# A decoder-layer step on one core: block sums and output-weight sums on VectorE, half of the weight steps moved to the second couples, stores on GpSimd's queue, and the first output weights loaded into operand places

## The chip, the core and the metric

The kernel runs on one core of a Trainium2 chip. The core has TensorE (PE, matmuls, with its weight loads shown as PEld), VectorE (DVE), ScalarE (ACT), GpSimd (POOL) and SyncE (SP), which here only issues transfers (DMAs). Every engine works through its own instructions in order. A DMA stands in the queue of the engine that issues it; an issue that has to wait for something holds up what stands behind it on that engine. The metric is the device time of one execution in microseconds (us).

## The reference

One step of a decoder layer on a prompt of 2048 rows and 8 sample rows, in float32, width 1024. Cut to what matters:

```python
hn = rmsnorm(x, g_norm) * (1 + scale) + shift           # scale, shift, gate from c @ w_ada + b_ada
z  = hn @ w_in                                          # (2048, 1024) @ (1024, 5136)
xa, za, q, k, v, glr, zg = split(z)
# group 1: conv4 over xa, two block-diagonal gates, a recurrence h = a*h + u, y_lru = h * silu(za)
# group 2: 4 heads of gated linear attention over chunks, with a state of 128x256 per head,
#          y_gla = rmsnorm(o) * silu(zg)
mix = concat([y_lru, y_gla]) @ w_out                    # (2048, 2048) @ (2048, 1024)
y   = rmsnorm(x + gate * mix, g_final)
```

The states of both groups are outputs too, and the 8 sample rows go through the same layer with states of their own (`state_gla` for group 2).

## The kernel before

Float32 products are made of two float32r parts, a high and a low one: x = hi + lo, three matmuls per product. A *split* makes them: ACT copies (`hi`), DVE subtracts (`lo`). The large products use a scheme with seven block products in place of eight (operands A11, A12, A21, A22 and their sums S1 to S4 on the row side; B11, B12, B21, B22 and combinations T1 to T4 on the weight side).

The prompt is worked on in two halves of 1024 rows. In order of time:

- **First-half heads** (to about 348 us): projections and attention of four heads (`gla_head`). Beside them run the row sums (`sums`, 40 additions on POOL into S1, S2 and, by way of memory, S3, S4), the gate (`ada_gate`), the second half's rows (`second_rows`, which normalizes them and stores eight row operands `fd`) and the gate weights.
- **First-half couples** (to about 628 us): eleven pairs of column blocks (eight `Lru`, three `Zg`), each seven products of 12 matmuls. `couples` interleaves the products of neighbours (list `uses`) and prepares each product's weights five uses ahead (`lead=5`) in one of seven places `op`. For the first half a couple loads raw weights (`load_raw`), splits them, and stores the parts to `wtd`; `combine` also multiplies the 8 sample rows with them (`sample_cols`, L303 and L309).
- **Second-half heads** (to about 939 us): as the first, with a tail of sample work (`sample_state`: loads `vsd` and `state_gla`, ACT scales, DVE adds). Beside them runs `out_weights`: 16 steps, each of which loads four blocks of `w_out` (tile `r`), multiplies them by the gate `g`, makes three sums (tile `t`) on POOL, splits two of them (tile `p`), and stores all to memory (`wd`, `wd2`) for the output projection.
- **Second-half couples** (to about 1166 us): the weights' parts come back from `wtd`.
- **Output projection** (to the end): seven products per pair of row blocks, weights from `wd`, `wd2` in the places `w0` to `w6` (`load_w`).

Work beside the main products is put off by `after(units, fn)` and called by `tick`, which counts the main line's progress; a product of a couple counts half a unit. `with behind(q)` gives an instruction the place behind the latest one of engine q; so `low_dma` puts a DMA behind what SP has at that time. A tile that is written again waits for all readers of its earlier use, stores among them. SP's and ACT's DMAs signal through eight semaphores in turn, so a ninth waits for the first.

Of the kernel before, what the change touches and what calls it, by code (L numbers as in the profile page):

```python
# [14 lines left out]
P = 128  # L15
# [38 lines left out]
def hybrid_kernel(ctx, tc, i, o):  # L54
# [64 lines left out]
    am = cp.tile([P, 4, P], F32, name="am")  # L119
    V.memset(am, 0.0)  # L120
    amh = cp.tile([P, 4, P], F32R, name="amh")
    aml = cp.tile([P, 4, P], F32R, name="aml")
# [10 lines left out]
    St = [cp.tile([P, DV], F32, name=f"S{h}") for h in range(H)]  # L133
# [3 lines left out]
    g2s = cp.tile([P, H * DK], F32R, name="g2s")  # L137
# [33 lines left out]
    gls = hnp.tile([P, TH + NS], F32R, name="gls")  # L171
# [192 lines left out]
    def take(col, n, k0, nk, raw):  # L364
# [6 lines left out]
        else:  # L371
# [4 lines left out]
            after(0.5, lambda: SP.dma_start(parts[col, k0], both[:, :, c].bitcast(F32)))  # L376
# [394 lines left out]
    def out_weights(hp, pp, then):  # L771


        def begin(q):

            g = hp.tile([P, 2, 256], F32, tag="g", name="g")
# [4 lines left out]
            r = load(8 * q)  # L781

            def add():
                G.tensor_tensor(g, g, bt, op=OP.add)
                step(8 * q, r, g)

            after(1, add)

        def where(s):

            return s // 8, s // 4 % 2, s % 4

        def load(s):
            q, f, m = where(s)
# [7 lines left out]
        def step(s, r, g):  # L802
            t = hp.tile([P, 3, 256], F32, tag="t", name="t", bufs=2)
            b11, b12, b21, b22 = r[:, 0, 0], r[:, 0, 1], r[:, 1, 0], r[:, 1, 1]
            q, f, m = where(s)
            c = slice(q * 256, q * 256 + 256)
            last = s % 8 == 7
            ahead = None if last else load(s + 1)

            def split(n, x):  # L810
                p = pp.tile([P, 2, 256], F32R, tag="p", name="p", bufs=2)
                with behind(S), behind(V):
                    S.copy(p[:, 0], x)
                    V.tensor_tensor(p[:, 1], x, p[:, 0].bitcast(F32), op=OP.subtract)
                return lambda: low_dma(wd2[2 * f + n, :, :, m, c], p.bitcast(F32))

            def store():
                for x, k in ((r.rearrange("p a b n -> p (a b) n"), 0), (t, 4)):
                    y = slice(1 - f, x.shape[1] - f)
                    low_dma(wd[f, k + y.start:k + y.stop, :, m, c].rearrange("k p n -> p k n"), x[:, y])  # L820

            for a in range(2):
                G.tensor_tensor(r[:, a], r[:, a], g, op=OP.mult)
            G.tensor_tensor(t[:, 1], b22, b12, op=OP.subtract)
            G.tensor_tensor(b12, b12, b11, op=OP.subtract)
            G.tensor_tensor(t[:, 0], b22, b12, op=OP.subtract)
            G.tensor_tensor(t[:, 2], b21, t[:, 0], op=OP.subtract)

            def splits():
                keep = split(0, b22 if f else b11), split(1, t[:, 2 * f])  # L830
                after(0.5, lambda: end(keep))

            def end(keep):
                for k in keep:
                    k()
                store()
                if not last:
                    step(s + 1, ahead, g)
                else:
                    after(1, (lambda: begin(1)) if q == 0 else then)  # L840

            after(1, splits)
# [221 lines left out]
    def sample_state(h, smp, b0, st, done, more):  # L1064
# [17 lines left out]
        after(0.5, update)  # L1082
        after(2.5, lambda: sample_out(h, b0, st, s0, done, more), True)

    def sample_out(h, b0, st, s0, done, more):
# [5 lines left out]
        SP.dma_start(o[7][0, b0:b0 + 4, h].rearrange("b k v -> k b v"), s0)  # L1091
# [28 lines left out]
    def sample_heads(k):  # L1120
# [15 lines left out]
        more = (lambda: after(0.5, lambda: sample_heads(k + 1))) if k < 3 else lambda: None  # L1136
# [1292 lines left out]
```

## Time and profile before

| | |
|---|---|
| median of 3 runs | 1507.06 us (1502.69 to 1511.88) |
| the profiled execution | 1506.31 us, its span 1504.3 us |
| PE idle, all of the span | 80.0 us |
| granted PE clock, mean | 0.981 |
| DMA | 340.84 MB, mean 227 GB/s |

The page gives for each engine its busy time, then the span in 40 equal slices of 37.6 us. In the two rows below, each digit is the share of a slice in tenths, 9 for 90% or more:

```profile
DVE  5776775665698888757778574667667686588886
POOL 1351602224313232054364100000002000000000
```

POOL's arithmetic lies in slices 1 to 4 (the sums), 5 to 16 (rows, couples' combinations) and 17 to 22 (the weight steps). DVE is at 8 or 9 in the first-half couples (slices 11 to 15). Further views of the trace are quoted with the prediction: waits (who waited for whom, total us, times, the longest), windows (for each stretch the busy time of the five engines PE, PEld, DVE, ACT, POOL, then granted clock, DMA share, GB/s), timelines (start, duration, engine, line, operation, and in brackets the idle time before it and what ended it), and sources (duration of one line's instructions in ns, least, median and most).

### The profile page before, as it was taken

What the parts mean: (1) busy time and instruction counts of PE and PEld (TensorE: products, weight loads), DVE (VectorE), ACT (ScalarE), POOL (GpSimd) and SP (SyncE); (2) the same over time, 40 slices, a digit from 0 to 9 for tenths busy, and PEclk for the clock granted to TensorE, in tenths of its full rate; (3) what the DMA queues carried; (4) which work ended last, traced back from release to release, by engine and by line L of the source; (5) the groups of instructions that cost most, each with busy time, mean ns of one, the idle gap of its engine ahead of it and who ended that gap; (6) DMA issues with size and microseconds to landing.
All of it is one profiled execution on the core that took longest, in us unless ns stands there. A gap on an engine that the chain in (4) does not pass through costs nothing.

```text
span 1504.3 us, 22504 instructions
## 1 busy us (share of the span) xinstructions
PE 1424.3 (95%) x8113; PEld 1175.7 (78%) x8113; DVE 1072.3 (71%) x2262; ACT 701.7 (47%) x1310; POOL 291.3 (19%) x297
## 2 busy tenths in 40 slices
PE   7989999997999999898999799999999899999997
PEld 5878889786777777778888788778888687777786
DVE  5776775665698888757778574667667686588886
ACT  4524344544675767433444332575663432244332
POOL 1351602224313232054364100000002000000000
PEclk9999999999999999999999899999999999999999
DMA  9625536748668548988878554766579857793452
GB/s 321 261 85 181 203 134 212 242 135 259 230 240 304 208 173 281 327 261 282 284 269 299 164 186 156 247 196 204 181 225 337 359 207 261 260 351 119 145 169 105
DMA packets 196469, 340.84 MB, mean 227 GB/s; under 512 B 12355, under 2 KB 130787, under 8 KB 192638
## 3 DMA queue, kind: packets, MB, share of 16 engines
q1 hardware_dynamic: 163061, 311.87, 60.6%
q10 hardware_dynamic: 31056, 20.19, 4.2%
q0 software_dynamic: 2240, 7.34, 1.2%
q8 instruction: 64, 1.05, 0.3%
q14 instruction: 48, 0.39, 0.1%
HBM read 204.73 MB, written 134.69 MB: 226 GB/s over the span
## 4 chain that ended last, share of the span: by engine, by line
PE 52%; DVE 15%; DMA 15%; issue 9%; ACT 5%; POOL 2%; SPq 1%; ACTq 0%; DVEq 0%; POOLq 0%
PE acc L2067 11%; PE tp L2067 8%; PE acc L1524 4%; PE tp L1524 3%; PE acc L701 3%; PE acc L702 3%; PE acc L703 3%; PE acc L397 2%; PE acc L396 2%; PE acc L395 2%; DMA raw<-in_w_in_dram 2%; DMA wd<-scratch 2%; DMA w<-wd 2%; PE po L1047 1%; DVE tg L1674 1%
## 5 line engine op out<-in xcount | busy, mean ns | idle before, releaser
L1524 PE MATMUL acc<-op,op 128*128 128x512 f32 x1056 | 251.4, 392 | 2.4 <-DMA op<-wtd 2.0
L1524 PEld LDWEIGHTS acc<-op,op 128*128 128x128 f32 x1056 | 198.3, 189 | 46.0 <-ACT op L1304 3.2
L1524 PE MATMUL tp<-op,op 128*128 128x512 f32 x792 | 197.6, 396 | 5.0 <-DVE acc L1534 5.0
L2067 PE MATMUL acc<-w,a 128*128 128x512 f32 (+1 forms) x792 | 189.6, 393 | 5.3 <-DMA w<-wd 4.1
L2067 PEld LDWEIGHTS acc<-w,a 128*128 128x128 f32 x792 | 148.5, 190 | 41.9 <-issue 7.9
L1524 PEld LDWEIGHTS tp<-op,op 128*128 128x128 f32 x792 | 148.6, 190 | 37.5 <-DVE acc L1534 5.9
L395 PE MATMUL acc<-w,op 128*128 128x256 f32 (+1 forms) x508 | 152.2, 300 | 3.2 <-ACT w L373 2.2
L397 PE MATMUL acc<-w,op 128*128 128x256 f32 (+1 forms) x508 | 146.2, 288 | 1.5 <-DVE op L270 1.5
L396 PE MATMUL acc<-w,op 128*128 128x256 f32 (+1 forms) x508 | 145.6, 287 | 0.8 <-DVE w L374 0.8
L2067 PE MATMUL tp<-w,a 128*128 128x512 f32 x564 | 137.2, 393 | 0.0
L2067 PEld LDWEIGHTS tp<-w,a 128*128 128x128 f32 x564 | 105.2, 188 | 28.0 <-issue 5.2
L701 PE MATMUL acc<-op,w 128*128 128x512 f32 x296 | 122.1, 412 | 2.3 <-ACT w L373 2.3
L702 PE MATMUL acc<-op,w 128*128 128x512 f32 x296 | 117.1, 396 | 0.0
L703 PE MATMUL acc<-op,w 128*128 128x512 f32 x296 | 117.0, 395 | 0.0
L395 PEld LDWEIGHTS acc<-w,op 128*128 128x128 f32 x508 | 98.1, 193 | 5.5 <-ACT w L373 2.6
L397 PEld LDWEIGHTS acc<-w,op 128*128 128x128 f32 x508 | 97.7, 192 | 2.1 <-DVE op L270 1.9
L396 PEld LDWEIGHTS acc<-w,op 128*128 128x128 f32 x508 | 97.6, 192 | 2.0 <-DVE w L374 1.1
L227 ACT ACTIVATE junk<-on 128x256 bf16<-128x256 f32 x64 | 26.7, 418 | 134.5 <-DVE on L1052 105.8
L1918 ACT CAST a<-s 128x512 fp32r<-128x512 f32 x61 | 36.5, 620 | 98.4 <-issue 35.8
L1641 DVE SCALAR_TENSOR_TENSOR cv<-xa,vecT,cv 128x512 f32<-128x512 f32 x96 | 73.1, 762 | 11.4 <-ACT cv L1639 10.3
L711 POOL DMA_DIRECT2D mixd<-zs x27 | 20.5, 761 | 304.4 <-DVE zs L1683 266.3
L1048 DVE TENSOR_TENSOR S<-S,pkv 128x256 f32<-128x256 f32 x60 | 25.1, 418 | 72.8 <-PE po L1047 72.4
(424 smaller groups left out, 2900.4 us busy)
## 6 DMA issues: line engine op xcount, KB each, us to landing
wtd<-op SPq DMA_DIRECT2D x77, 512.0 KB
op<-wtd SPq DMA_DIRECT2D x77, 512.0 KB
w<-parts SPq DMA_DIRECT2D x16, 1024.0 KB
a<-mixd SPq DMA_DIRECT2D x63, 256.0 KB
parts<-w SPq DMA_DIRECT2D x15, 1024.0 KB
w<-wd SPq DMA_DIRECT2D x10, 1024.0 KB
wr<-in_w_in_dram SPq DMA_DIRECT2D x18, 512.0 KB
wada<-in_w_ada_dram SPq DMA_DIRECT2D x16, 512.0 KB
```

The lines of the kernel that those rows point to most:

```text
L227: S.activation(junk[:m, :n], x, AF.Square, accum_out=out)
L395: PE.matmul(ps, part(0, kt, c), hi[:, kt % 4], start=kt == 0, stop=False)
L396: PE.matmul(ps, part(0, kt, c), lo[:, kt % 4], start=False, stop=False)
L397: PE.matmul(ps, part(1, kt, c), hi[:, kt % 4], start=False, stop=kt == KT - 1)
L701: PE.matmul(ps[:, :n], hi[:, kt], a, start=kt == 0, stop=False)
L702: PE.matmul(ps[:, :n], hi[:, kt], b, start=False, stop=False)
L703: PE.matmul(ps[:, :n], lo[:, kt], a, start=False, stop=kt == KT - 1)
L1048: V.tensor_tensor(St[h], St[h], pkv, op=OP.add)
L1524: PE.matmul(ps, w[:, u, k], t[:, v, k], start=q < 3 and (k, u, v) == (0, 0, 0), stop=(k, u) == (3, 1), skip_group_check=True)
L1641: V.scalar_tensor_tensor(cv, xa[:, k:k + 512], cw[k], cv, op0=OP.mult, op1=OP.add)
L1918: S.copy(t[:, 0, k], (low(t) if src is None else src)[:, k])
L2067: PE.matmul(ps, t[:, u, k], w[:, v, k, c], start=(q < 3 or ps is own) and (k, u, v) == (0, 0, 0), stop=(k, u) == (3, 1), skip_group_check= ...
```

## The change

Line numbers of the changed kernel are higher by 1 to 41.

- `sums`: its 40 additions go from POOL to DVE, cut into pieces half a unit apart; its stores `sd` go from SP to POOL's queue.
- `out_weights` takes f: the eight steps of f = 0 stay beside the second-half heads (their stores on POOL's queue), the eight of f = 1 run beside the second-half couples (their stores on SP's, tiles in a pool of their own, one buffer `t` in place of two). The arithmetic is on DVE in both.
- Stores that move to POOL's queue: `parts`, `fd`, `sd`, `gated_w`, the sample states `o[7]`, the states `o[4]`. In all POOL issues 127 DMAs in place of 28, SP 605 in place of 684, ACT 61 in place of 77; POOL has 108 tensor operations of two inputs in place of 246, DVE 1199 in place of 1059.
- `second_rows` starts behind `ada_gate`, and its first step waits for the sums (`ready`).
- `couples`: couple 1's raw weights are asked for behind four uses' weights, and its sample columns come behind product 1. One of the `zs` of `Zg(0, 0)` gets a tile of its own.
- Sample states are used 1 unit (was 0.5) and 3 units (was 2.5) after their loads are asked for.
- Output weights: the places are those of the couples' operands (`ops`, tags o0 to o6), free by then; the first weight B11 is loaded behind product (10, 0) of the second-half couples. Small tiles of the projection move into earlier pools.

```diff
-            after(0.5, lambda: SP.dma_start(parts[col, k0], both[:, :, c].bitcast(F32)))
+            after(0.5, lambda: G.dma_start(parts[col, k0], both[:, :, c].bitcast(F32)))
...
-            for a in range(2):
-                G.tensor_tensor(r[:, a], r[:, a], g, op=OP.mult)
-            G.tensor_tensor(t[:, 1], b22, b12, op=OP.subtract)
...
+        def step(q, m, r, g):
+            t = hp.tile([P, 3, 256], F32, tag="t", name="t", bufs=2 - f)
...
+            with behind(V):
+                for a in range(2):
+                    V.tensor_tensor(r[:, a], r[:, a], g, op=OP.mult)
+
+            def combine():
+                with behind(V):
+                    V.tensor_tensor(t[:, 1], b22, b12, op=OP.subtract)
+                    V.tensor_tensor(b12, b12, b11, op=OP.subtract)
+                    V.tensor_tensor(t[:, 0], b22, b12, op=OP.subtract)
+                    V.tensor_tensor(t[:, 2], b21, t[:, 0], op=OP.subtract)
+                after(0.5, high)
...
+            def store(ps):
+                put = low_dma if f else G.dma_start
...
+                    after(0.5 if f else 1, lambda: step(q, m + 1, ahead[0], g))
...
-        after(0.5, update)
-        after(2.5, lambda: sample_out(h, b0, st, s0, done, more), True)
+        after(1, update)
+        after(3, lambda: sample_out(h, b0, st, s0, done, more), True)
...
-        SP.dma_start(o[7][0, b0:b0 + 4, h].rearrange("b k v -> k b v"), s0)
+        G.dma_start(o[7][0, b0:b0 + 4, h].rearrange("b k v -> k b v"), s0)
...
-            S.dma_start(fd[0:4, :, k, p * P:(p + 1) * P].rearrange("o p c -> p o c"), f)
+            G.dma_start(fd[0:4, :, k, p * P:(p + 1) * P].rearrange("o p c -> p o c"), f)
...
-            after(1, lambda: SP.dma_start(fd[4:8, :, k, p * P:(p + 1) * P].rearrange("o p c -> p o c"), b))
+            G.dma_start(fd[4:8, :, k, p * P:(p + 1) * P].rearrange("o p c -> p o c"), b)
...
-            add_up(s1, [(h21, None), (h22, OP.add), (l21, OP.add), (l22, OP.add)])
-            add_up(s2, [(s1, None), (h11, OP.subtract), (l11, OP.subtract)])
+            with behind(V):
+                add(s1, h21, h22)
+                add(s1, s1, l21)
...
         def zs(self):
-            if self.more:
-                return self.more.pop(0)()
+            own = self.more.pop(0) if self.more else None
+            if own:
+                return own()
...
         cs[0].load_raw()
-        for u in range(lead):
+        for u in range(lead - 1):
             prepare(u, True)
+        cs[1].load_raw()
+        if cs[1].src is not None:
+            prepare(lead - 1)
         for u, (m, q) in enumerate(uses):
             cs[m].product(q)
...
+            if u == 1 and cs[1].src is None:
+                prepare(lead - 1)
             prepare(u + lead)
...
+    zg0 = Zg(0, 0)
+    zg0.more = [None] * 3 + [lambda: lp.tile([P, 512 + 4], F32, tag="xa", name="zs")[:, :512]]
...
+    after(3, lambda: out_weights(1, owp, owp, lambda: lp.tile([P, 2, 256], F32, tag="t2", name="g"), lambda: done.append(1)))
...
-    couples([Lru(1, j) for j in range(KT)] + [Zg(1, h) for h in HEADS[:2]] + [end], at={(0, 0): lambda: low_op(1, S3, fd[6]), (0, 1): lambda: low_op(1, S4, fd[7]),
-                                                (0, 6): lambda: low_dma(o[4][0, 0, HEADS[3]], St[HEADS[3]]), (9, 2): early_rows})
+    couples([Lru(1, j) for j in range(KT)] + [Zg(1, h) for h in HEADS[:2]] + [end], at={(0, 0): lambda: low_op(1, S4, fd[7]),
+                                                (0, 6): lambda: low_dma(o[4][0, 0, HEADS[3]], St[HEADS[3]]), (9, 2): open_pre, (10, 0): early_w(B11, 0)})
```

Three places show how instructions move. First TensorE at the start of the first-half couples. L303 and L309 (L304 and L310 in the changed kernel) are the sample columns of couples 0 and 1, L1524 (L1549) the products, 12 matmuls each. Before:

```order
L1112 MATMUL tp<-ident,on 128x128 x8
L303 MATMUL acc<-raw,fs 32x256 x2
L254 MATMUL tp<-ident,scratch 128x128 x4
L303 MATMUL acc<-raw,fs 32x256 x6
L309 MATMUL acc<-sel_113,tmp 128x8 x2
L303 MATMUL acc<-raw,fs 32x256 x8
L1524 MATMUL acc<-op_149,op 128x512 x12
L1524 MATMUL tp<-op_1189,op 128x512 x12
```

and in the changed kernel:

```order
L1113 MATMUL tp<-ident,on 128x128 x8
L304 MATMUL acc<-raw,fs 32x256 x8
L1549 MATMUL acc<-op_146,op 128x512 x12
L1549 MATMUL acc<-op_1185,op 128x512 x7
L310 MATMUL acc<-sel_113,tmp 128x8 x2
L1549 MATMUL acc<-op_1185,op 128x512 x2
L1549 MATMUL tp<-op_1186,op 128x512 x2
L1549 MATMUL acc<-op_1185,op 128x512 x2
L1549 MATMUL tp<-op_1186,op 128x512 x10
L1549 MATMUL acc<-op_1185,op 128x512
L304 MATMUL acc<-raw,fs 32x256 x8
L1549 MATMUL acc<-op_147,op 128x512 x12
```

The second eight of L303, on couple 1's raw weights, stood ahead of the first product; three products (36 matmuls) now stand ahead of them, and couple 0's turn (L310) lies among these.

Second, SP's queue in the last of the second-half heads. L769 are the stores of a weight step, L799 (L795) its loads, L1071 and L1073 (L1072 and L1074) the loads for the samples. Before:

```order
L799 DMA scratch<-in_w_out_dram 128x2x256 x2
L370 DMA w<-parts 128x2x1024
L769 DMA wd_67<-p 256x1x256 x2
L769 DMA wd<-scratch 128x3x256
L769 DMA wd<-scratch 128x2x256
L1071 DMA scratch<-vsd 128x1024
L799 DMA scratch<-in_w_out_dram 128x2x256 x2
L1073 DMA scratch<-in_state_gla_dram 128x4x256
```

and in the changed kernel:

```order
L371 DMA w<-parts 128x2x1024
L795 DMA scratch<-in_w_out_dram 128x2x256 x2
L1074 DMA scratch<-in_state_gla_dram 128x4x256
L1072 DMA scratch<-vsd 128x1024
L1074 DMA scratch<-in_state_gla_dram 128x4x256
L371 DMA w<-parts 128x2x1024 x2
```

The weight steps' stores are gone from between the loads; a load of output weights still stands ahead of a state's.

Third, SP's queue in the second-half couples. L1463 (L1488) are the loads of the couples' weights from `wtd`, the others there gate weights. Before:

```order
L1463 DMA op<-wtd 128x1024 x7
L769 DMA amh<-gw 128x512
L1463 DMA op<-wtd 128x1024 x7
L769 DMA aml<-gw 128x512
L1463 DMA op<-wtd 128x1024 x7
```

and in the changed kernel:

```order
L1488 DMA op<-wtd 128x1024
L795 DMA r<-in_w_out_dram 128x2x256 x2
L770 DMA wd_67<-p 256x1x256
L1488 DMA op<-wtd 128x1024 x3
L770 DMA wd_67<-p 256x1x256
L770 DMA wd<-r 128x3x256
L770 DMA wd<-t 128x2x256
L1488 DMA op<-wtd 128x1024
L795 DMA r<-in_w_out_dram 128x2x256 x2
L770 DMA aml<-gw 128x512
L1488 DMA op<-wtd 128x1024 x3
```

Between four loads of `op` there now stand four stores and two loads of a weight step.

More of the change, by code (lines that the diff above doesn't have):

```diff
@@ L827, in step @@
[L827 to L838, printed above, removed]
-                else:
-                    after(1, (lambda: begin(1)) if q == 0 else then)
-            after(1, splits)
+                    put(wd[f, k + y.start:k + y.stop, :, m, c].rearrange("k p n -> p k n"), x[:, y])
@@ L1326, in step @@
         def step(p, x, k):
+            if p == 0 and not ready:
+                after(0.5, lambda: step(p, x, k))
+                return
             pt = turn(x, (k, k + 4))
@@ L1365, in one @@
             (h11, l11), (h21, l21), (h22, l22) = [high_low(op, k) for op in (A11, A21, A22)]
[L1366 to L1373 removed]
+            with behind(V):
+                add(s1, h21, h22)
+                add(s1, s1, l21)
@@ new lines, in more, with high, low @@
+            def more():
+                with behind(V):
+                    add(s1, s1, l22)
+                    add(s2, s1, h11, OP.subtract)
+                    add(s2, s2, l11, OP.subtract)
+                after(0.5, high)
+            def high():
+                with behind(S):
+                    for op, x in ((S1, s1), (S2, s2)):
+                        S.copy(place[op][:, 0, k], x)
+                other(k, s2, low)
+            def low():
+                with behind(V):
+                    for op, x in ((S1, s1), (S2, s2)):
+                        t = place[op]
@@ L1374, in split, with other, last @@
                         V.tensor_tensor(t[:, 1, k], x, t[:, 0, k].bitcast(F32), op=OP.subtract)
-            after(2, split)
-            after(1.5, lambda: other(k, s2))
-        def other(k, s2):
+            after(0.5, more)
+        def other(k, s2, low):
             s3, s4 = two()
             (h11, l11), (h21, l21), (h12, l12) = [high_low(op, k) for op in (A11, A21, A12)]
-            add_up(s4, [(h12, None), (s2, OP.subtract), (l12, OP.add)])
-            add_up(s3, [(h11, None), (h21, OP.subtract), (l21, OP.subtract), (l11, OP.add)])
+            with behind(V):
+                add(s4, h12, s2, OP.subtract)
+                add(s4, s4, l12)
+            def last():
+                with behind(V):
+                    add(s3, h11, h21, OP.subtract)
+                    add(s3, s3, l21, OP.subtract)
+                    add(s3, s3, l11)
+                after(0.5, store)
+                after(0.5, (lambda: one(k + 1)) if k < 3 else lambda: None)
@@ L1384, in store @@
             def store():
                 for x, n in ((s3, 0), (s4, 1)):
-                    SP.dma_start(sd[n, :, k], x)
-            after(1.5, store)
-            after(*((0.5, lambda: one(k + 1)) if k < 3 else (1.5, then)))
+                    G.dma_start(sd[n, :, k], x)
+                if k == 3:
+                    then()
+            low()
+            after(0.5, last)
         new_op(0, S1)
@@ L2286, in hybrid_kernel @@
         SP.dma_start(x.lo(A22), x.rows(1, 1))
-    for q in range(2):
-        load_w(0, q, q)
     def first_loads():
-        load_w(0, T1, 2)
+        with behind(SP):
+            load_w(0, T1, 2)
         x1.s[S3] = part(1)
```

187 lines of the change are left out of this document (95 added, 92 removed).

## The prediction

> **What bounds the kernel now.** I read the head of the page first, then TensorE's waits, then windows around the longest of them, then timelines of the queues behind them.
>
> ```profile
> span 1504.3 us, 22504 instructions
> PE 1424.3 (95%) x8113; PEld 1175.7 (78%) x8113; DVE 1072.3 (71%) x2262; ACT 701.7 (47%) x1310; POOL 291.3 (19%) x297
> ```
>
> TensorE (PE) is busy 95% of the span. The work on it stays the same, so the change can gain only from its 80 us of idle time (1504.3 less 1424.3) and from the time at which its clock is halved. TensorE's waits (who waited for whom, total, times, longest) are few and large:
>
> ```profile
> PE pkv L1039 <- ACT kTh L1022: 10.5, 3, 8.5
> PE acc L303 <- DMA raw<-in_w_in_dram: 6.6, 3, 5.4
> PE tp L1524 <- DVE acc L1534: 5.0, 2, 4.8
> PE acc L2067 <- DMA w<-wd: 4.1, 1, 4.1
> ...
> PE acc L309 <- ACT tmp L304: 2.3, 1, 2.3
> PE acc L701 <- ACT w L373: 2.3, 1, 2.3
> ```
>
> Each of the four longest is followed by a stretch at a granted clock (first number after the five engines) of about half:
>
> ```profile
> 353.00:360.40 7.40, 3.63 (x20) 2.15 (x21) 3.70 (x7) 3.07 (x6) 4.94 (x5) 0.54 0.87 247
> 616.40:623.20 6.80, 6.15 (x15) 4.79 (x16) 4.68 (x7) 2.48 (x3) 0.00 (x0) 0.50 1.04 337
> 838.30:848.50 10.20, 4.53 (x21) 4.53 (x22) 6.93 (x28) 3.56 (x9) 1.78 (x3) 0.50 0.73 246
> 1169.40:1176.20 6.80, 5.58 (x13) 4.45 (x14) 0.00 (x0) 0.00 (x0) 0.63 (x1) 0.50 0.98 406
> ```
>
> Half a clock over 6.8 us costs 3.4 us, over 10.2 us 5.1 us. I count these with the stalls.
>
> **The change part by part.** Term B, start of the first couples:
>
> ```profile
> 347.84 1.75 SPq L1454 DMA_DIRECT2D raw<-in_w_in_dram  x2
> ...
> 350.81 0.61 PE L309 MATMUL acc<-sel,tmp 128*128 128x8 f32 x4 [2.30 <-ACT tmp L304]
> 356.77 1.93 PE L303 MATMUL acc<-raw,fs 128*32 128x256 f32 x16 [5.35 <-DMA raw<-in_w_in_dram]
> ```
>
> Couple 1's raw weights are issued at 347.84, behind row stores on SP, and TensorE's sample columns of couple 1 (L303) stand ahead of the first product. In the changed order three products stand before these columns, and the row stores have left SP for POOL. The 5.35 us have nothing left to wait for; the 2.30 us in front (ACT's copy) need not go, and if they stay they may keep the half clock. Ends 0 (the products' own operands are no sooner) and 11.05 (5.35 + 2.30 + 3.4); I take **8**, between 5.35 and 11.05.
>
> [...] The wait of 2.29 us at L701 (2.3 in the list above) ended at 286.26, and the clock behind it was:
>
> ```profile
> 285.30:292.10 6.80, 5.84 (x14) 4.60 (x15) 4.14 (x16) 5.38 (x8) 0.00 (x0) 0.50 1.05 344
> ```
>
> [...]
>
> Term C, last first-half couples:
>
> ```profile
> 602.44 0.39 ACTq L711 DMA_DIRECT2D mixd<-zs  x1
> 612.60 0.60 ACT L1117 ACTIVATE zs<-tp 128x512 f32<-128x512 f32 x1 [5.80 <-DMA mixd<-zs]
> 617.05 5.49 PE L1524 MATMUL tp<-op,op 128*128 128x512 f32 x12 [4.78 <-DVE acc L1534]
> ```
>
> ACT waits for a buffer `zs` until the store issued at 602.44 lands; behind it in ACT's queue stand the copies that free the accumulators. The change gives the fourth `zs` a tile of its own, so this wait has nothing left to wait for. 4.78 + 3.4 = 8.2; what is late next is DVE's sum, which ACT alone delayed. Ends 0 and 8.2; I take **8**.
>
> Term D, second-half heads:
>
> ```profile
> 821.25 3.73 SPq L769 DMA_DIRECT2D wd<-scratch  x2
> ...
> 831.09 1.29 SPq L799 DMA_DIRECT2D scratch<-in_w_out_dram  x2
> 832.43 0.59 SPq L1073 DMA_DIRECT2D scratch<-in_state_gla_dram  x1
> ```
> ```profile
> SPq L799 <- DMA wd<-scratch: 32.6, 12, 5.4
> ```
> ```profile
> 839.08 1.70 ACT L1079 ACTIVATE scratch<-scratch,smp 128x256 f32<-128x256 f32 x4 [8.50 <-DMA scratch<-in_state_gla_dram]
> ```
>
> SP's queue stops at a load of output weights (L799) that waits for an earlier store's landing, and the state load behind it starts at 832.43. ACT, in order, waits 8.50 us for that state, and TensorE 8.5 us for ACT. After the change the stores of this half are on POOL's queue, only half as many steps run here, and the state's use comes half a unit later. 8.5 + 5.1 = 13.6. Next late is ACT's `kTh`, with its other two waits (2.0 together). Ends 0 (the store's landing still gates the load) and 13.6; I take **12**.
>
> Term E, start of the output projection:
>
> ```profile
> 1158.88 1.59 SPq L1929 DMA_DIRECT2D w<-wd  x2
> ```
> ```profile
> 1170.62 7.66 PE L2067 MATMUL acc<-w,a 128*128 128x512 f32 x21 [4.06 <-DMA w<-wd]
> ```
> ```profile
> PE acc L2067 <- DVE w L1921: 1.2, 1, 1.2
> ```
>
> The first weights (2 MB in two loads) are asked for at 1158.88, when their place comes free. Now the first one is asked for behind product (10, 0), nine products before the couples' end at 1166.5; a product takes 2.7 us (the 5.49 us of 12 matmuls above at half clock, halved), so at about 1142, 17 us sooner. 4.06 + 3.4 + 1.2 = 8.7; the second weight has one product more to land in. Ends 0 and 8.7; I take **8**.
>
> The moved arithmetic:
>
> ```profile
> L823 POOL TENSOR_TENSOR scratch<-scratch x32: 1262/1294/2208, 648.6 to 835.8; 128x512 f32<-128x512 f32 x32
> ```
> ```profile
> L1646 DVE TENSOR_TENSOR xl<-cv,xh x32: 678/684/694, 376.0 to 1119.3; 128x512 fp32r<-128x512 f32 x32
> ```
> ```profile
> L1048 DVE TENSOR_TENSOR S<-S,pkv x60: 402/420/425, 97.7 to 913.3; 128x256 f32<-128x256 f32 x60
> ```
> ```profile
> 69.00:190.00 121.00, 110.36 (x891) 96.14 (x890) 86.58 (x202) 44.20 (x102) 57.06 (x41) 0.97 0.44 155
> 940.00:1084.00 144.00, 141.84 (x631) 114.95 (x632) 96.87 (x137) 90.91 (x135) 7.68 (x10) 1.00 0.64 208
> 1084.00:1166.50 82.50, 82.39 (x367) 67.30 (x365) 59.34 (x91) 42.05 (x66) 12.21 (x17) 1.00 0.81 275
> 1200.00:1225.00 25.00, 25.00 (x111) 20.47 (x110) 23.43 (x37) 11.70 (x22) 0.00 (x0) 1.00 0.41 147
> ```
>
> The 40 sums cost 40 x 0.684 = 27.4 us of DVE between about 69 and 190, which fills it to (86.58 + 27.4)/121 = 94%. At 94% (23.43 of 25, last row) TensorE lost nothing. On the other side POOL's arithmetic leaves, and with it DVE's longest instances (POOL's own operation ran 1262 to 2208 ns in contention). TensorE's whole idle time there is 10.6 us. So the heads' term has ends -5 (half of that goes) and +10 (it doubles); I take **0**. The half-as-many weight steps among the second-half heads are cheaper for DVE than the sums, since their splits were on it before; they go with this.
>
> The other eight weight steps now run among the second-half couples. A step is 2 x 0.684 + 6 x 0.420 = 3.89 us of DVE, eight are 31.1, and two additions of the gate 1.4: 32.5 us. DVE goes from 96.87 to 129 of 144 us, 90%, under the 94% above. A step also moves 1664 KB (512 loaded, 512 + 384 + 256 stored): 13.6 MB more over 144 us, 208 to 302 GB/s, a little over the 275 at which TensorE was busy 82.39 of 82.5 us. Its six transfers stand on SP among the loads `op<-wtd`, asked for five products (13.6 us) ahead; a wait for a store cost SP 2.7 us on average (32.6/12). The single buffer `t` adds a wait to DVE's next combination: behind it stand the couple's sums that free accumulators, and TensorE waits for those. Ends 0 (all fits) and 32.5 (every DVE microsecond delays TensorE); nearest rows say 0, but several new waits meet here, so I take **+8**, 1 us a step.
>
> POOL's stores:
>
> ```profile
> L711 POOL DMA_DIRECT2D mixd<-zs x27: 752/752/925, 977.1 to 1169.3; - x27
> ```
>
> These stores, the row stores and sums among them, are issued by POOL, at 752 ns each; POOL is busy 19%, less its arithmetic now, so I cost that at nothing. If stores wait there, D's 13.6 comes back.
>
> The sum, against the profiled execution's own 1506.31 us (2.0 around the span; the median of the three runs is 1507.06): 1506.3 - 8 - 8 - 12 - 8 + 0 + 8 = **1478**.
>
> **The rivals.**
>
> 1. VectorE becomes the bound among the second-half couples: the whole 32.5 us is paid, 1506.3 - 36 + 32.5 = 1503. For it: the couples' sums and the scan share DVE with it in order. Against: 90% is not full.
>
> 2. Each stall is half replaced by the next wait: 1506.3 - 18 + 8 = 1496. For it: the waits are long chains (SP, then a transfer, then ACT, then PE). Against: in each, what the next wait depends on was done before.
>
> 3. Slower: the six transfers per step on SP hold back `op<-wtd`. A step's r load waits for the store of its own buffer, as L799 does above, where the longest such wait was 5.4 us; on SP everything behind it waits too, the prefetches first. If that uses up the 13.6 us of lead and 5.4 us reach TensorE in each of eight steps, with a half clock of 3.4 behind each, it costs 8 x 8.8 = 70: 1506.3 - 36 + 70 = 1540. It decides from 36/8 = 4.5 us lost per step. For it: transfers take longer at 302 GB/s. Against: a lead of 13.6 us is more than twice 5.4.
>
> 4. POOL's stores starve and D returns: 1478 + 13.6 = 1492. For it speaks no row here: issues took 752 to 925 ns while DVE was busy 67% (96.87 of 144). [...]
>
> **How the numbers follow.** A measurement of this kernel can tell about 0.5%, 7.5 us, from no change: 1499.5 to 1514.6 is "same". Chances: my forecast (1460 to 1490) 0.62; rival 1, 0.10 (same); rival 2, 0.12 (faster); rival 3, 0.08 (slower); rival 4, 0.05 (faster); still better than 1460, 0.03. So faster 0.82, same 0.10, slower 0.08. Low end: all stalls whole, 11.05 + 8.2 + 13.6 + 8.7 = 41.6, heads -5, couples 0: 1460. High end: couples 32.5: 1503. That leaves out rival 3, what is below 1460 and mishaps of rival 1 beyond its price.
>
> **What would show it.** TensorE's waits without L303 behind raw weights, without DVE's `acc` near 612, without `kTh` of 8.5 us, and without `w<-wd`, and the granted clock 1.00 at those places: terms B to E. TensorE's busy share in the second-half couples: 98% (141.84 of 144) now, a percentage point for each 1.4 us of my 8; waits there by DVE speak for rival 1, by `op<-wtd` for rival 3. Issues of POOL's stores well over 925 ns, or landings that ACT waits for, speak for rival 4. I am wrong if DVE's share in the couples passes 94% or TensorE's idle total stays near 80 us.

## The result, and the profile after

The changed kernel takes 1481.64 us (median of 4 runs, 1479.71 to 1483.43) beside 1507.18 us; the ratio is 0.9843, 95% interval 0.9825 to 0.9861. Run again later beside the kernel before, it was 0.9817 (0.9790 to 0.9844). The forecast, 1478 us, stands for 0.981.

The head of the page, engines busy (share of the span), and DVE and POOL in 40 slices:

```profile
span 1480.1 us, 22516 instructions
PE 1417.9 (96%) x8113; PEld 1172.7 (79%) x8113; DVE 1098.0 (74%) x2402; ACT 699.0 (47%) x1310; POOL 212.2 (14%) x258
...
DVE  5767975658788888756767864788866886688886
POOL 0200154334313222001111100000002000000000
```

TensorE does the same 8113 matmuls and is idle 62.2 us (1480.1 less 1417.9) where it was idle 80.0; its busy time is 6.4 us shorter, at a mean granted clock of 0.988 in place of 0.981. DVE took on 26 us and POOL gave off 79. TensorE's waits now, in the columns of before (the products of the couples, L1524 before, are L1549, and those of the projection, L2067 before, are L2117, so line numbers differ by more than the 41 given above):

```profile
PE tp L1014 <- DVE xb L1262: 5.3, 1, 5.3
PE tp L255 <- DVE am L1018: 4.3, 1, 4.3
PE tp L1014 <- ACT ob L1220: 3.7, 1, 3.7
PE tp L864 <- DVE g L854: 3.6, 1, 3.6
PE acc L1549 <- DMA op<-wtd: 3.6, 1, 3.6
...
PE acc L1549 <- DVE op L1496: 2.5, 1, 2.5
PE tp L1549 <- DVE acc L1559: 2.3, 2, 2.1
```

Of the four long waits of before, three are gone and DVE's `acc` (term C) has shrunk from 4.8 to 2.1 us. The first five are new, or were under 3 us. So the gain is a difference of two sums, and the windows by stage show where each lies. The stages end at the first product of a group of couples or at the end of its last; in a row stand the stretch, its length, and the busy time of PE first. Before, then after:

```profile
0.00:358.64 358.64, 326.73 (x2545) 279.93 (x2545) 236.10 (x665) 158.78 (x333) 106.80 (x129) 0.96 0.59 198
358.64:628.35 269.71, 257.05 (x1210) 201.35 (x1207) 215.49 (x315) 173.65 (x265) 67.04 (x42) 0.98 0.72 253
628.35:922.97 294.62, 275.73 (x1867) 243.25 (x1865) 202.15 (x628) 112.08 (x282) 95.72 (x98) 0.98 0.72 236
922.97:1166.56 243.59, 240.88 (x1071) 195.66 (x1069) 164.32 (x240) 138.58 (x208) 19.95 (x27) 1.00 0.72 238
1166.56:1170.62 4.06, 0.00 (x2) 0.03 (x1) 1.38 (x2) 0.60 (x1) 1.28 (x2) 0.85 1.02 427
1170.62:1504.30 333.68, 323.90 (x1432) 255.51 (x1432) 252.90 (x415) 118.01 (x222) 0.53 (x1) 0.99 0.61 217
```
```profile
0.00:342.90 342.90, 322.68 (x2525) 277.57 (x2525) 236.39 (x695) 153.97 (x327) 85.76 (x140) 0.98 0.58 203
342.90:610.80 267.90, 254.73 (x1230) 199.06 (x1227) 226.71 (x325) 177.21 (x272) 73.95 (x46) 1.00 0.73 256
610.80:899.50 288.70, 276.42 (x1867) 245.74 (x1865) 194.83 (x665) 108.92 (x268) 30.95 (x43) 0.98 0.60 202
899.50:1148.30 248.80, 242.60 (x1071) 196.70 (x1069) 185.62 (x304) 140.16 (x222) 19.56 (x27) 0.99 0.89 298
1148.30:1480.10 331.80, 321.49 (x1433) 253.60 (x1431) 254.47 (x417) 118.73 (x223) 1.96 (x3) 0.99 0.61 215
```

The first-half heads are 15.7 us shorter, their couples 1.8, the second-half heads 5.9; the second-half couples are 5.2 us longer; the wait of 4.1 us ahead of the projection is gone, and the projection is 1.9 shorter. Together 24.2, the difference of the spans. About 1.6 us of the heads' 15.7 have only moved: twenty matmuls of sample columns now lie behind the couples' first product (PE x2545 and x2525 in the first rows). The second-half couples begin at 922.97 before, not near 939 as given above.

### The profile page after: what moved, and what is told of

It reads as the page before. It is cut to its first block, busy times and chain, and to the rows that moved or that the text cites. A ratio compares the mean times of both kernels' runs of the same rounds, so it can differ in the third digit from the quotient of the medians.

```text
span 1480.1 us, 22516 instructions
## 1 busy us (share of the span) xinstructions
PE 1417.9 (96%) x8113; PEld 1172.7 (79%) x8113; DVE 1098.0 (74%) x2402; ACT 699.0 (47%) x1310; POOL 212.2 (14%) x258
## 4 chain that ended last, share of the span: by engine, by line
PE 52%; DVE 15%; DMA 9%; ACT 5%; issue 4%; SPq 0%; ACTq 0%; DVEq 0%
PE acc L2117 11%; PE tp L2117 8%; PE acc L1549 6%; PE tp L1549 4%; PE acc L704 3%; PE acc L702 3%; PE acc L703 3%; DVE tg L1700 2%; PE acc L396 2%; PE acc L397 2%; PE acc L398 2%; DMA raw<-in_w_in_dram 1%; DVE op L1496 1%; DVE cv L1667 1%; DVE tx L1698 1%
## 5 line engine op out<-in xcount | busy, mean ns | idle before, releaser
L1549 PE MATMUL acc<-op,op 128*128 128x512 f32 x1056 | 252.3, 393 | 6.1 <-DMA op<-wtd 3.6
L1549 PEld LDWEIGHTS acc<-op,op 128*128 128x128 f32 x1056 | 198.2, 189 | 49.5 <-DMA op<-wtd 4.0
L1549 PE MATMUL tp<-op,op 128*128 128x512 f32 x792 | 196.1, 393 | 2.3 <-DVE acc L1559 2.3
L2117 PE MATMUL acc<-w,a 128*128 128x512 f32 (+1 forms) x792 | 187.2, 389 | 1.8 <-DVE w L1982 1.8
L2117 PEld LDWEIGHTS acc<-w,a 128*128 128x128 f32 x792 | 146.7, 188 | 37.6 <-issue 3.4
L1549 PEld LDWEIGHTS tp<-op,op 128*128 128x128 f32 x792 | 146.9, 188 | 34.4 <-DVE acc L1559 3.2
L2117 PE MATMUL tp<-w,a 128*128 128x512 f32 x564 | 137.2, 393 | 0.0
L2117 PEld LDWEIGHTS tp<-w,a 128*128 128x128 f32 x564 | 105.2, 188 | 27.9 <-issue 5.2
L1049 DVE TENSOR_TENSOR states<-states,pkv 128x256 f32<-128x256 f32 x60 | 25.0, 417 | 58.3 <-PE po L1048 58.0
L704 PEld LDWEIGHTS acc<-op,w 128*128 128x128 f32 x296 | 55.9, 189 | 12.2 <-DVE w L375 0.2
```

The costliest lines, as they stand in the source:

```text
L704: PE.matmul(ps[:, :n], lo[:, kt], a, start=False, stop=kt == KT - 1)
L1549: PE.matmul(ps, w[:, u, k], t[:, v, k], start=q < 3 and (k, u, v) == (0, 0, 0), stop=(k, u) == (3, 1), skip_group_check=True)
L2117: PE.matmul(ps, t[:, u, k], w[:, v, k, c], start=(q < 3 or ps is own) and (k, u, v) == (0, 0, 0), stop=(k, u) == (3, 1), skip_group_check= ...
```

## The experiments

All were compared with the kernel before on the same chip; the ratio's 95% interval is in the table. The stages are as above, in us, from each run's profiled execution, beside those of the first and the repeated run of the changed kernel.

| run | ratio to before | heads 1 | couples 1 | heads 2 | couples 2 | rest |
|---|---|---|---|---|---|---|
| before | 1 | 358.6 | 269.7 | 294.6 | 243.6 | 337.7 |
| changed | 0.9843 (0.9825 to 0.9861) | 342.9 | 267.9 | 288.7 | 248.8 | 331.8 |
| changed, again | 0.9817 (0.9790 to 0.9844) | 343.3 | 267.6 | 287.6 | 249.4 | 329.5 |
| a1 old couple start | 0.9848 (0.9823 to 0.9874) | 341.9 | 272.8 | 285.5 | 249.5 | 329.5 |
| a2 first steps' stores on SP | 0.9788 (0.9758 to 0.9819) | 341.1 | 268.9 | 279.2 | 252.4 | 329.4 |
| a3 no early weight | 0.9823 (0.9797 to 0.9848) | 342.6 | 268.8 | 286.1 | 243.4 | 335.5 |
| a4 sums on POOL | 0.9932 (0.9908 to 0.9956) | 358.8 | 270.3 | 287.4 | 249.5 | 333.6 |
| b2 no `zs` tile | 0.9841 (0.9813 to 0.9870) | 341.2 | 273.4 | 287.2 | 250.0 | 330.5 |
| d1 = a2, early state | 0.9803 (0.9773 to 0.9833) | 340.1 | 268.6 | 284.8 | 249.5 | 330.2 |
| d2 = a2, sixteen steps | 1.0038 (1.0018 to 1.0057) | 341.4 | 269.2 | 295.2 | 275.9 | 329.5 |
| d3 = a2, sixteen short steps | 0.9944 (0.9921 to 0.9967) | 341.6 | 268.6 | 300.8 | 257.4 | 329.4 |
| e1 = a2, rows after sums | 0.9781 (0.9759 to 0.9802) | 335.0 | 275.5 | 278.0 | 250.3 | 329.5 |
| c1 = a2, no early weight, late gate | 0.9764 (0.9738 to 0.9790) | 341.3 | 269.1 | 275.5 | 247.9 | 333.8 |
| c3 = a2, early weight later, late gate | 0.9743 (0.9724 to 0.9762) | 342.5 | 269.2 | 275.3 | 247.5 | 329.8 |

### The changed kernel again

> The changed kernel itself, as the base for the others on the same chip: a ratio of 0.984 to the kernel before, as measured first.

0.9817, a little better than the first time; the intervals overlap. Its stages differ from the first run's by at most 2.3 us, so a difference of 3 us or more in one stage of an experiment is read as its own, a smaller one is not.

### a1: the old order at the couples' start (term B)

```diff
-        for u in range(lead - 1):
+        for u in range(lead):
             prepare(u, True)
-        cs[1].load_raw()
-        if cs[1].src is not None:
-            prepare(lead - 1)
...
-            if u == 1 and cs[1].src is None:
-                prepare(lead - 1)
```

> The changed kernel, with the old order at the start of the couples: couple 1's first weights are prepared with the first five, so that its sample columns stand ahead of the first product again. Changed kernel: 1481.6 us. Theory 1 (the order removed the stall of term B): TensorE waits again for couple 1's raw weights or for ACT ahead of the first product, 5 us or more, with a half clock behind it: about +8, 1490 us. Theory 2 (it was enough that the row stores left SP's queue, so that the raw weights come early): no such wait, 1481.6 within 2 us.

The couples are 5 us longer, the heads 1 us shorter. No wait for raw weights came back: with the row stores off SP's queue the weights are there. TensorE waits for splits of couple 0's weights instead. TensorE's timeline of a1 (start, duration, operation, and in brackets the idle time and what ended it):

```profile
341.92 3.02 PE L1549 MATMUL acc<-op,op 128*128 128x512 f32 x12
347.38 0.74 PE L1549 MATMUL tp<-op,op 128*128 128x512 f32 x2 [2.44 <-ACT op L1495]
351.22 4.63 PE L1549 MATMUL tp<-op,op 128*128 128x512 f32 x10 [3.11 <-DVE op L1496]
```

and of the changed kernel, which waits once:

```profile
349.10 1.43 PE L1549 MATMUL acc<-op,op 128*128 128x512 f32 x5 [2.50 <-DVE op L1496]
```

So theory 2 holds for the load. By the stages the couples end 4 us later than in the changed kernel, of which 1.7 us are a stretch of half clock from 605.1 to 608.5, behind term C's wait; that leaves 2 to 3 us for the order (the ratios, 0.9848 beside 0.9817 and 0.9843, are too close to show it). (The raw weights of couple 1 were always asked for with the first preparation; the added call of `load_raw` finds them asked for. What moves is the preparation of couple 1's first weights and its sample columns.)

### a2: the first eight steps' stores on SP (term D)

```diff
-                put = low_dma if f else G.dma_start
+                put = low_dma
```

> The changed kernel, with the stores of the eight weight steps beside the second-half heads on SP's queue in place of POOL's. Theory 1 (the stores' place on SP made the stall of term D): a state load stands behind a load that waits for a store, ACT waits over 6 us for it, TensorE over 5 us: +8 to +13, 1490 to 1495 us. Theory 2 (half as many steps and the later use of the state are enough): no such wait, and as stores by SP land sooner than by POOL, the wait of 5.3 us near 729 (SP stood 11.0 us behind a store by POOL) shrinks: 1475 to 1482 us.

Faster by 4 to 8 us by the ratios, with an interval that overlaps the repeated run's: the second-half heads fall from 288.7 and 287.6 to 279.2 us, of which the couples give back 3 to 4. No wait of term D came back, so theory 1 is out; the median, 1473.1 us, is 2 us below theory 2's range. The changed kernel's new wait of 5.3 us is gone, but not for the reason that theory 2 gives. SP's queue in the changed kernel:

```profile
709.05 0.34 SPq L1072 DMA_DIRECT2D scratch<-vsd  x1
720.44 1.21 SPq L795 DMA_DIRECT2D scratch<-in_w_out_dram  x2
721.70 0.59 SPq L1298 DMA_DIRECT2D op<-fd  x1
```

and ACT's timeline:

```profile
728.90 1.04 ACT L1305 CAST op<-op 128x1024 fp32r<-128x1024 f32 x1 [6.88 <-DMA op<-fd]
```

A load of output weights stands 11 us for the store of its own buffer `r`, which POOL issued; the load of a row operand behind it comes late, ACT's split waits for that in order, and behind it DVE and TensorE. It is the chain of term D with another load at its end. SP's waits of this kind in the second-half heads (total, times, longest), in the changed kernel and in a2:

```profile
SPq L795 <- DMA wd<-scratch: 38.0, 4, 11.8
```
```profile
SPq L795 <- DMA wd<-scratch: 8.1, 4, 4.1
```

SP waits less in a2, yet the row operand is asked for no sooner, and ACT waits for it still. SP and ACT in a2, then ACT in c3 (below), which has these stores on SP too:

```profile
722.62 0.66 SPq L1298 DMA_DIRECT2D op<-fd  x1
731.52 2.00 ACT L1305 CAST op<-op 128x1024 fp32r<-128x1024 f32 x2 [2.35 <-DMA op<-fd]
```
```profile
732.92 2.00 ACT L1305 CAST op<-op 128x1024 fp32r<-128x1024 f32 x2 [8.04 <-DMA op<-fd]
```

The split's place in ACT's order has moved with the edit. In the changed kernel it stands ahead of the head's copies `kTh` and `amh` (L1023, L1020), as in a1, a3, a4 and b2; in a2 and c3 it stands behind them, as in d1, e1 and c1. In c3 ACT waits longer than in the changed kernel, and TensorE has no wait of 1 us near it. So the wait of 5.3 us went because less stood behind the late split; what the stores' landing by itself is worth isn't shown.

### d1: the sample states used early again (term D)

```diff
-        after(1, update)
-        after(3, lambda: sample_out(h, b0, st, s0, done, more), True)
+        after(0.5, update)
+        after(2.5, lambda: sample_out(h, b0, st, s0, done, more), True)
```

> The kernel with the first eight weight steps' stores on SP (ratio 0.9788 to the kernel before), and the sample states used 0.5 and 2.5 units after their loads are asked for, as before the change. Theory 1 (the later use is what keeps term D's stall away): TensorE waits 4 us or more behind ACT's wait for a state, with a half clock: +5 to +13 us on 0.9788. Theory 2 (half as many steps suffice): within 2 us of it.

The ratio moved by 0.0015, within both intervals, and no long wait came back; the second-half heads of the profiled run are 5.6 us longer. The one new wait over 1 us in them is of 2.29 us near 728, with 1.7 us of half clock. With half the steps, the later use is not what keeps D's stall away; whether it is worth a few us stays open.

### d2 and d3: all sixteen steps beside the heads

```diff
+    def second_weights():
+        after(1, lambda: out_weights(1, ow, owp, lambda: ow.tile([P, 2, 256], F32, tag="g"), lambda: low_op(1, S1, fd[4], units=2)))
+
-    after(0.5, lambda: out_weights(0, ow, owp, lambda: ow.tile([P, 2, 256], F32, tag="g"), lambda: low_op(1, S1, fd[4], units=2)))
+    after(0.5, lambda: out_weights(0, ow, owp, lambda: ow.tile([P, 2, 256], F32, tag="g"), second_weights))
...
-    after(3, lambda: out_weights(1, owp, owp, lambda: lp.tile([P, 2, 256], F32, tag="t2", name="g"), lambda: done.append(1)))
+    done.append(1)
```

This is d3, with steps of 2 units (combination at once, store with the lower parts); d2 has steps of 2.5 units and loads S1's rows between the halves.

> As the kernel with the first eight steps' stores on SP (0.9788), but all sixteen weight steps stand beside the second-half heads, 2.5 units each, on DVE; none stands beside the second-half couples. Theory 1 (the move of half the steps is needed; the heads can't hold sixteen): SP's loads wait for stores again, TensorE waits of over 4 us come back among the heads: +6 to +15 us. Theory 2 (the steps cost where DVE is slowed by POOL, and on DVE the heads hold them): within 3 us of 0.9788, with 2 us less of TensorE's idle time in the couples.

The whole gain was lost. Of the 16 us by which the heads are longer than a2's, 13.0 are one wait at their end: the heads' last matmul ends 282.2 us after the first-half couples (279.4 in a2), and then TensorE waits for the first weights of the second-half couples. The steps did not end with the heads, and what was left fell on the couples' start, where TensorE waits for couple weights and for a row operand:

```profile
PE acc L1549 <- DMA op<-wtd: 23.2, 3, 13.0
PE acc L1549 <- ACT op L1305: 13.4, 1, 13.4
```

So in d2 the heads' own work was hardly slower with steps of 2.5 units; the steps were too many to end in time. d3 repeats the question with shorter steps.

> All sixteen weight steps beside the second-half heads again, on DVE and with stores on SP, but in steps of 2 units, so that they end well ahead of the couples (in d2 they did not, and row loads fell into the couples). Theory 1 (the heads can't hold sixteen steps, so moving half is a part of the gain): TensorE waits of 5 us and more among the heads again, heads 8 to 15 us longer than in the kernel with stores on SP (279.5 us from the last first-half product to the first second-half product): ratio 0.985 to 0.990. Theory 2 (it was POOL's arithmetic; on DVE the heads hold all): within 3 us of 0.9788.

The heads are 21.6 us longer than a2's, 5.1 of them a wait for couple weights at their end, and the ratio rises by 0.0156. The heads' window in d3, then in a2 (fourth busy time from the left: ACT; third: DVE):

```profile
610.20:911.00 300.80, 280.67 (x1866) 248.70 (x1864) 220.40 (x731) 113.44 (x282) 7.71 (x11) 0.96 0.71 235
```
```profile
610.00:889.20 279.20, 273.08 (x1867) 243.07 (x1865) 194.61 (x665) 108.98 (x268) 7.79 (x11) 0.99 0.61 208
```

DVE is not full (220.4 of 300.8). The waits that came are those of chains: DVE in order for the load of a step, TensorE for DVE (5.1 us) and ACT (2.7), and each brings a stretch of 6.8 us at half clock. Theory 1 holds, by more than it said: sixteen steps beside the heads cost 38 us (d2) and 23 us (d3) beside a2 by the ratios, so the second-half heads' gain stands on half of them being elsewhere. Two things stay open: d3's steps are shorter too, and the 8.5 us wait for `kTh` itself came back neither in d2 nor in d3 (2.7 us at the most), so no run undoes one edit and brings it back.

### a3: no early load of the first output weight (term E)

```diff
-                                                (0, 6): lambda: low_dma(o[4][0, 0, HEADS[3]], St[HEADS[3]]), (9, 2): open_pre, (10, 0): early_w(B11, 0)})
+                                                (0, 6): lambda: low_dma(o[4][0, 0, HEADS[3]], St[HEADS[3]]), (9, 2): open_pre})
...
+    load_w(0, B11, 0)
     load_w(0, T2, 1)
```

> The changed kernel without the early load of the first output weight: it is loaded behind the couples, as the second is. Theory 1 (the early load removed the stall of term E, and itself made the 3.6 us wait for couple weights near 1129): that wait and its half clock go, -5.3, and the wait for the output weights at the start of the projection comes back with its half clock, +6 to +9: 1482 to 1486 us. Theory 2 (the operand places alone, free earlier, were enough): no wait at the start of the projection, and without the one near 1129 the kernel is 1476 us.

Even, and between the two theories: 1477.8 us. The second-half couples (the window begins and ends 0.4 us late):

```profile
897.90:1141.40 243.50, 241.32 (x1071) 195.51 (x1070) 185.22 (x304) 140.69 (x222) 20.12 (x27) 1.00 0.88 298
```

Without the early load they take 243.4 us with all eight weight steps among them, 243.6 before without any. So the steps cost nothing there on balance, at 298 GB/s and with DVE busy 185 of 243.5 us; the 5.2 us that the changed kernel's couples lost are the early load's, which stands in front of two loads of `op`. The stall at the projection's start did not come back whole either. SP asks for the first two weights at

```profile
1127.18 1.63 SPq L1924 DMA_DIRECT2D w<-wd  x2
```

13.7 us before the projection starts at 1140.9, and TensorE doesn't wait. Before it was 11.7 us (1158.88 to 1170.62), 4.06 of them a wait. By the code this is the operand places, which are free at once; no run puts the old places back. The projection then takes 4 to 6 us longer than with the early load, by small waits for splits and a stretch of half clock behind one of 1.8 us, which the changed kernel has without the half clock.

### b2: no tile of its own for `zs` (term C)

```diff
-    zg0.more = [None] * 3 + [lambda: lp.tile([P, 512 + 4], F32, tag="xa", name="zs")[:, :512]]
```

> The changed kernel without the tile of its own for a `zs` of Zg(0, 0). Theory 1 (that tile is what shortened the stall of term C, from 4.78 to 2.08 us without a half clock behind it): ACT waits again for a store's landing near 600, TensorE 4 to 5 us with a half clock: +4 to +6 us on the changed kernel. Theory 2 (the stall was shortened since the order of splits moved): within 1 us of the changed kernel.

TensorE's wait for DVE's `acc` is 4.5 us again, with a stretch of 3.4 us at half clock behind it: theory 1. The couples are 5.5 us longer, but 1.7 of that are a half clock behind term B's wait, which has nothing to do with this tile. The ratio moved by 0.0024 only, within the intervals. The rest of the wait, 2.1 us, isn't the store's: DVE's own row of work (a scan of 2.28 us ahead of the sum) sets it.

### a4: the sums on POOL again

```diff
         def add(x, a, b, sign=OP.add):
-            V.tensor_tensor(x, a, b, op=sign)
+            G.tensor_tensor(x, a, b, op=sign)
```

> The changed kernel with the 40 additions of the sums back on POOL, in the same small pieces. The first-half heads took 5 us less than the prediction's terms explain. Theory 1 (the additions' move to DVE is worth nothing for TensorE, the gain is from what else moved): 1481.6 within 2 us. Theory 2 (POOL's additions held back DVE, as its longest instances show, and through it TensorE): +4 to +7, 1486 to 1489 us, with TensorE waits of some 2 us between 75 and 100.

13 to 17 us slower (0.9932 beside 0.9843 and 0.9817), nearly all in the first-half heads, 358.8 us, and more scattered (1486.8 to 1501.4; the profiled execution is the slowest). DVE's timeline of a4, four scans of the decay:

```profile
141.50 5.49 DVE L964 TENSOR_TENSOR_SCAN xb<-xb 128x128 f32<-128x128 f32 x4
```

while POOL adds:

```profile
141.00 5.71 POOL L1362 TENSOR_TENSOR scratch<-scratch,op 128x512 f32<-128x512 f32 x4
```

Four scans without POOL's arithmetic beside them took 1.95 us (a2):

```profile
282.63 1.95 DVE L964 TENSOR_TENSOR_SCAN xb<-xb 128x128 f32<-128x128 f32 x4
```

A scan's median is 415 ns in the changed kernel and 417 in a4, its longest 759 and 1451. ACT waits 6.5 us for what follows these scans, and TensorE 6.6 us for ACT. Theory 2 holds in its direction, at twice its price. From 66 to 100 us TensorE is busy 32.3 us in the changed kernel, 28.0 in a4 and 27.1 before, so some 4 us go with the sums on POOL in either kernel. The rest isn't the place of the additions alone: before, with its stores on other queues, POOL did the same sums, and the heads were at their end, where term B's waits began, at 348.5. What the stores in POOL's order add to it was not taken apart.

### e1: the rows after the sums, as before

```diff
-            ready = []
-            sums(sc2, lambda: ready.append(1))
-            ada_gate(sc2, lambda: second_rows(sc2, ready, lambda: load_op(0, S3, sd[0])()))
+            ready = [1]
+            left = [lambda: second_rows(sc2, ready, lambda: load_op(0, S3, sd[0])()), lambda: None]
+            sums(sc2, lambda: left.pop()())
+            ada_gate(sc2, lambda: left.pop()())
```

> The kernel with the first eight steps' stores on SP, and the second half's rows started only when both the gate and the sums are done, as before the change. Theory 1 (the new TensorE waits of 4 us near 224 and 287 among the first-half heads come from the rows' earlier start): they go, -4 to -8 us to there, and as the rows end later, 2 to 6 us of it come back as a wait at the couples' start. Theory 2 (they come from the sums on DVE): they stay, and the rows end later: 0 to +5 us on 0.9788.

As theory 1 said: the heads are 6.1 us shorter than a2's, without the waits near 224 and 287 (one of 3.2 us near 268 came), and the couples 6.6 longer. The rows' earlier start moves a loss and doesn't remove it.

### c1 and c3: what the runs point to

```diff
-            after(1.5, add)
+            after(1.5 if f or q else 2.5, add)
...
-                                                (0, 6): lambda: low_dma(o[4][0, 0, HEADS[3]], St[HEADS[3]]), (9, 2): open_pre, (10, 0): early_w(B11, 0)})
+                                                (0, 6): lambda: low_dma(o[4][0, 0, HEADS[3]], St[HEADS[3]]), (9, 2): open_pre, (9, 6): early_w(B11, 0)})
```

This is c3, on a2; c1 has no early load.

> The changed kernel with three edits that the runs point to: the first eight weight steps' stores on SP (0.9788 alone), no early load of the first output weight (its gain at the projection's start and its loss in the couples were even), and the first gate addition of the weight steps one unit later, so that DVE doesn't wait for its load near 632 (3 to 4 us and half a clock of 1.7). Theory 1 (the three add up): 0.975 to 0.977. Theory 2 (each frees only what the next wait takes): 0.979 or more, with a new TensorE wait of over 2 us among the heads.

> As c1, but the first output weight is asked for behind product (9, 6), four products later than in the changed kernel, in place of not early at all. If the wait for couple weights near 1129 came from the 2 MB load in front of two loads of `op`, one of them is still behind it: a wait of at most 2 us there, and no waits for weights at the projection's start: 0.974 to 0.977, below c1. If the load's place doesn't matter: as the changed kernel there, 3 us or more of wait, and no better than c1.

c1 is 0.9764, in the range of its theory 1, and c3 0.9743 (median 1465.6 us beside 1504.9): c3 beats the changed kernel's 0.9843 and 0.9817 clear of all intervals, c1 and c3 overlap. The wait near 632 is gone in both and nothing took its place: the heads are 275 us. In c3 the wait for couple weights is still 3.2 us, more than the 2 that were expected, but the projection keeps its 4 us. Its TensorE waits:

```profile
PE tp L1014 <- ACT ob L1220: 3.8, 1, 3.8
PE tp L255 <- DVE am L1018: 3.5, 1, 3.5
PE tp L1549 <- DMA op<-wtd: 3.2, 1, 3.2
```

## Why the prediction was right

The time was right and the likeliest case came. But the working was right by sums, not term by term, and that the errors nearly cancelled is luck.

One error runs through B to E: the prediction took half the length of a stretch of half clock as its price. But the end of each wait lies in the stretch and is counted already; what runs slower is TensorE's work in it (12 matmuls took 5.49 us at 617.05, 2.88 us at 481.15 at full clock). The prediction's own rows have 3.63, 6.15, 4.53 and 5.58 us of work in the four stretches, so the price was 1.8, 3.1, 2.3 and 2.8 us, not 3.4, 3.4, 5.1 and 3.4. The whole stalls were 9.5, 7.9, 10.8 and 8.1 us, and D's 12 was more than there was to gain.

- **B**, 8 predicted. Before: 7.65 us of waits and 1.8 of clock; after: 2.50 us and no half clock. 7.0 gone, 1.7 of it by luck: in a2 the same wait, 2.49 us, has a stretch of 3.4 us at half clock behind it. a1 shows that the cause was two edits: the row stores off SP (no wait for raw weights in any order), and the order, 2 to 3 us.
- **C**, 8 predicted, 5.8 measured (4.78 to 2.08 us, and 3.1 of clock). The step that failed: "what is late next is DVE's sum, which ACT alone delayed". DVE's own work delayed it by 2 us more.
- **D**, 12 predicted, and its stall of 10.8 did go, but the second-half heads gained only 5.9 us. The step that failed named the stores' place on POOL's queue among the reasons and put POOL's stores at nothing: a2 shows that this place costs 4 to 8 us, in the changed kernel by the same chain with a row operand at its end. d3 shows what carries the gain, half as many steps (21.6 us), and d1 that the later use isn't it. Which edit alone ends the 8.5 us wait stays open.
- **E**, 8 predicted, 5.9 measured (4.1 of the wait, 1.9 in the projection). a3 shows that the wait ends without the early load, so it is the places, as far as the code tells. (The first weights are 2 MB each, not 2 MB in two loads.)
- **The couples**, +8 predicted, +5.2 measured, and the cause is another. The steps cost 0 (a3: 243.4 beside 243.6); the sum's nearest rows had said so, and I put 1 us a step on top. DVE's busy time there rose by 21 us, to 75% of the stage (185.62 of 248.80): the steps' own instructions last 32.4 us in all, as I had counted, but they overlap with others. The 5.2 are from the early load, which the sum had at nothing: I named no work that it would delay.
- **The heads**, 0 predicted between -5 and +10, and about -1 measured, by two sizes of 5 that cancelled and that I had not worked out apart. The first-half heads gained 5.5 us beyond B (15.7, less 7.65 of waits and 0.9 of clock that are B's in that stage and 1.6 of moved columns): a4 shows the sums' move worth 13 to 17 us beside the other edits, and waits of 4.3 and 3.7 us with their clock, from the rows' start (e1), gave part of it back. The second-half heads gained 4.9 us less than D's 10.8: new waits of 3.6 and 5.3 us cost 13.4 with their clock, and five waits of 1.1 to 1.7 us that went gave 7.4 back.

As measured, 7.0 + 5.8 + 10.8 + 5.9 + 0.6 - 5.2 = 24.9 us, beside 28 forecast; the spans differ by 24.2.

Of the rivals, 1 and 3 did not come: eight steps in the couples held back TensorE by nothing that a3 can show. Rival 2 is partly what happened in the second-half heads. Rival 4 came by half: a wait behind POOL's store took 7 us back (5.3, and 1.5 of clock). Not by slow issues, though; the issues of the steps' stores in ns, and their landings (least, median, most):

```profile
L837 POOL DMA_DIRECT2D wd<-scratch x16: 725/761/939, 637.1 to 821.4; - x16
...
DMA to landing us min/median/max: 2.8/6.3/9.6
```

The issues took 725 to 939 ns here while DVE was busy 67% (194.83 of 288.70; 69% before); what made landings take up to 9.6 us, no row here shows.

## What to carry to other kernels

Follow a stall to the load or store at its end, and ask what stands behind that in an in-order queue. Moving the stores to POOL's queue left waits for their landing (up to 11.8 us) on SP; what spared TensorE in a2 and c3 is that little stood behind the late operand's split on ACT. Half of the steps in another stage, where TensorE's work is long and regular, cost nothing there (243.4 us with them in a3, 243.6 before). An early transfer of 2 MB is work too (the second-half couples took 248.8 us with it, 243.4 without), and has to be set against the loads that it stands in front of. Small arithmetic on an engine with nothing to do isn't free if it holds up another engine's instructions, as POOL's additions did DVE's scans in a4; the longest instances of a line show this better than its median (1451 ns in a4 beside 759, medians 417 and 415).

## What was not expected of the hardware

The half clock doesn't follow the length of a wait in these runs. In the changed kernel the wait of 2.50 us that ended at 349.10 had no half clock behind it; in a2 the same wait, 2.49 us, had 3.4 us of it; in c1 a wait of 1.45 us had 6.8. What differs in the rows below is where the wait falls. Before and in the changed kernel the stretches of half clock last 3.4, 6.8 or 10.2 us (the span's end cuts the last one off), and in the kernel before those at 353.59, 616.41, 838.28 and 1169.37 start 262.82, 221.87 and 331.09 us apart: 77, 65 and 97 times 3.413, a third of the 10.24 us that the one at 838.28 lasts. Stretches of 3.4 us that start such multiples away from a half clock, of the changed kernel, of a2 and of c1 (first TensorE's busy time; granted clock third from the right; c1's second row is two of them):

```profile
344.60:348.00 3.40, 2.00 (x9) 1.29 (x7) 3.40 (x3) 1.76 (x4) 3.32 (x3) 1.00 0.73 206
348.00:351.40 3.40, 2.30 (x12) 2.00 (x13) 3.40 (x5) 2.04 (x4) 2.11 (x2) 1.00 0.99 369
```
```profile
344.80:348.20 3.40, 0.91 (x4) 0.77 (x5) 3.40 (x4) 2.42 (x5) 2.70 (x3) 1.00 0.96 340
348.20:351.60 3.40, 3.40 (x12) 2.82 (x11) 3.12 (x6) 1.99 (x2) 0.79 (x1) 0.50 0.94 294
```
```profile
990.20:993.60 3.40, 1.72 (x7) 1.14 (x7) 2.38 (x5) 2.52 (x5) 0.00 (x0) 1.00 0.83 235
993.60:1000.40 6.80, 6.80 (x21) 5.46 (x20) 2.76 (x5) 5.95 (x9) 0.00 (x0) 0.50 0.95 325
```

In a2 the wait lies in one stretch, which leaves TensorE 0.91 us of work in 3.4, and half clock follows; in the changed kernel the border of two stretches cuts the same wait in two, 2.00 and 2.30 us of work are left, and none follows. In c1 1.72 us are left, the 1.45 us and smaller waits together, and half clock follows. These are three cases; when the clock is halved in general isn't shown. By them, as an estimate, a wait of 2 us here costs between 2 and 5.4 us (by c1's 6.8 us at half clock), and a change that moves it in time can pay or gain 3.4 us without touching it.
